# Q and out with eight heads on 128 partitions: 8 KB rows and an accumulated pair of matmuls in a linear attention kernel

## The chip, the core and the metric

One core of one Trainium2 chip. The metric is device time of one launch in microseconds (us). The profiled span runs from the first to the last instruction and is 1.7 to 1.9 us shorter than the timed run. With one core there is no other core to compare a run with; where a run is marked slow below, it lies over 1.5% above the fastest of its kernel. All ratios use fast runs.

## The reference

```python
batch, heads, seq, dim = 8, 12, 512, 64          # 96 heads, fp32
Q_feat, K_feat = np.maximum(0, Q), np.maximum(0, K)
KV    = np.einsum('bhkd,bhkv->bhdv', K_feat, V)  # 64x64 per head
K_sum = np.sum(K_feat, axis=2)
out   = einsum(Q_feat, KV) / (einsum(Q_feat, K_sum)[..., None] + 1e-10)
```

Q, K and V are 12.6 MB each, so is the output: 50.3 MB pass through the DMA engines, for little arithmetic.

## The kernel before

Four heads make a group; there are 24. GpSimd issues the loads, which cast fp32 to bf16 on the way. In Q and out each partition holds 16 positions of a head, 1024 values: rows of 4 KB in HBM. K and V rows are 2 KB. A group goes through VectorE (ReLU of K, V into a block-diagonal tile), TensorE (KV with a column of ones for the denominator), ScalarE (KV to bf16), TensorE (Q transposed), ScalarE (ReLU), TensorE (the product, one matmul per 32 output partitions) and VectorE (two normalizations of 128x512), then a store.

```python
# ... loads: K, V, Q of each group in turn; the last two Q at the very end
def mm_out(g):
    for j in range(2):
        po = pou.tile([P, 2, 512], fp32, name="ps_out")
        ps_out[g, j] = po
        for v in range(U // 2):
            u = j * (U // 2) + v
            for h in range(NHG):                      # four heads, 32 partitions each
                hs = slice(32 * h, 32 * h + 32)
                nc.tensor.matmul(po[hs, ...], qt[g][:, u, hs],
                                 kvd[g % NB][:, h // 2, h % 2, :, :], start=True, stop=True, ...)
# ...
for g in range(NG):
    mm_kv(g); evac_kv(g)
    if g + 1 < NG:
        prep(g + 1)                                   # ReLU of K, V copies (VectorE)
    if g > 0:
        mm_out(g - 1)
        store(g - 1, norm(g - 1))                     # groups 17 to 21: queued behind the loads
    transp(g); evac_qt(g)
mm_out(NG - 1)
store(NG - 1, norm(NG - 1))                           # in two halves
```

## Time and profile before

| | before |
|---|---|
| time, median | 131.77 us (131.31 to 132.03, four runs) |
| profiled span | 130.2 us |
| DMA packets, HBM bytes | 20126; 50.3 MB |
| TensorE matmuls, mean granted clock | 1344; 0.81 |
| last load packet ends | 119.9 us |
| VectorE ends its last normalization | 126.07 us |

The page cuts the span into 40 slices and gives each a digit for how busy an engine was; groups of instructions carry the busy time, the mean of one, and what ended the idle time before them. The packet records of the trace are read beside it: each has a queue, a size, a start and a duration, and they give the time of the last load. They are put on the span's clock to about 0.2 us. The queue that carries the engines' instructions is a line that the prediction passed over:

```profile
q8 instruction: 10, 0.16, 0.5%
```

Ten packets of 16 KB: the program itself is read by DMA.

### The profile page before, as it was taken

The numbers are of one execution on the slowest core, as the hardware profiler recorded it, in microseconds if no ns is written. First come the engines' busy times: TensorE is split into PE (matmuls) and PEld (weight loads), VectorE is DVE, ScalarE is ACT, GpSimd is POOL, SyncE is SP. The second block draws the span as 40 slices with busy tenths as digits, with TensorE's granted clock in tenths as the row PEclk, the third lists the DMA queues.
The fourth block names the chain that finished last, engine by engine and source line by source line (L and its number), as shares of the span: only waits on it lengthen the run. The fifth ranks groups of instructions, "written<-read, shape, count | busy, mean of one in ns | idle before, by whom it ended". The sixth has DMA issues, their size and how long they took to land.

```text
span 130.2 us, 3249 instructions
## 1 busy us (share of the span) xinstructions
PE 75.7 (58%) x1344; PEld 62.8 (48%) x1344; DVE 90.3 (69%) x228; ACT 43.7 (34%) x73; POOL 51.4 (39%) x81
## 2 busy tenths in 40 slices
PE   0057975648475574763843943954757658959510
PEld 0057863536455454543733832843745546757300
DVE  4388995837577577577685775775866859979860
ACT  1205554152323523423343244235132352535500
POOL 6986451414434335144344353352433433312100
PEclk9999999586865797698699599599596586777985
DMA  3999999999999999999999999999999999999982
GB/s 122 301 208 208 203 195 218 306 223 278 216 272 257 232 285 242 247 285 218 271 274 216 285 253 236 286 235 255 281 213 279 266 223 207 204 217 374 380 322 89
DMA packets 20126, 32.18 MB, mean 247 GB/s; under 512 B 1552, under 2 KB 13328, under 8 KB 20112
## 3 DMA queue, kind: packets, MB, share of 16 engines
q0 software_dynamic: 16688, 20.98, 87.3%
q1 hardware_dynamic: 3152, 10.49, 21.4%
q10 hardware_dynamic: 272, 0.52, 1.1%
q8 instruction: 10, 0.16, 0.5%
q14 instruction: 4, 0.03, 0.1%
HBM read 37.75 MB, written 12.58 MB: 387 GB/s over the span
## 4 chain that ended last, share of the span: by engine, by line
DMA 79%; DVE 7%; POOL 5%; issue 3%; PE 1%; ACT 1%; ACTq 0%; POOLq 0%
DMA v_sb<-in_V_dram 37%; DMA k_sb<-in_K_dram 23%; DMA q_sb<-in_Q_dram 19%; DVE o_sb L172 3%; DVE vbd L120 2%; POOL v_sb L83 2%; POOL k_sb L81 2%; DVE rec L171 1%; POOL q_sb L87 1%; ACT qt L147 1%; DVE den L169 1%; PE ps_out L158 1%; DVE kf L114 0%; PE ps_qt L143 0%; POOL ident masks.py:199 0%
## 5 line engine op out<-in xcount | busy, mean ns | idle before, releaser
L128 PE MATMUL ps_kv<-vbd,kf 128*128 128x130 bf16 x384 | 36.8, 270 | 40.1 <-DVE vbd L120 40.1
L128 PEld LDWEIGHTS <-kf 128*128 128x128 bf16 x384 | 33.6, 124 | 42.3 <-issue 28.6
L137 ACT CAST kvd<-ps_kv 64x260 bf16<-64x260 f32 x48 | 17.9, 374 | 49.6 <-PE ps_kv L128 49.0
L172 DVE TENSOR_TENSOR o_sb<-ps_out,rec 128x512 f32<-128x512 f32 x48 | 33.2, 692 | 1.7
L147 ACT ACTIVATE qt<-ps_qt 128x1024 bf16<-128x1024 bf16 x24 | 24.6, 1023 | 27.4 <-PE ps_qt L143 27.3
L120 DVE COPY vbd<-v_sb 64x1024 bf16<-64x1024 bf16 x46 | 19.9, 432 | 12.8 <-DMA v_sb<-in_V_dram 12.5
L158 PE MATMUL ps_out<-kvd,qt 128*32 128x130 bf16 x768 | 23.2, 271 | 8.2 <-DVE o_sb L172 5.3
L87 POOL DMA_DIRECT2D q_sb<-in_Q_dram x24 | 13.6, 565 | 31.3 <-DMA k_sb<-in_K_dram 30.2
L114 DVE TENSOR_SCALAR kf<-k_sb 128x2048 bf16<-128x2048 bf16 x23 | 16.0, 696 | 13.3 <-DMA k_sb<-in_K_dram 13.2
L81 POOL DMA_DIRECT2D k_sb<-in_K_dram x23 | 17.1, 743 | 18.6 <-DMA v_sb<-in_V_dram 16.7
L158 PEld LDWEIGHTS <-qt 128*32 128x32 bf16 x768 | 15.2, 115 | 15.0 <-DVE o_sb L172 7.8
L83 POOL DMA_DIRECT2D v_sb<-in_V_dram x23 | 17.3, 752 | 10.9 <-DMA q_sb<-in_Q_dram 9.2
L143 PE MATMUL ps_qt<-ident,q_sb 128*128 128x128 bf16 x192 | 18.8, 256 | 0.1
L143 PEld LDWEIGHTS <-q_sb 128*128 128x128 bf16 x192 | 14.2, 116 | 3.9 <-issue 2.6
L171 DVE RECIPROCAL rec<-den 128x8 f32<-128x8 f32 x48 | 9.8, 203 | 1.6
L169 DVE TENSOR_SCALAR den<-ps_out 128x8 f32<-128x8 f32 x48 | 7.7, 161 | 1.3 <-PE ps_out L158 0.6
L182 POOL DMA_DIRECT2D out_dram<-o_sb x5 | 2.9, 579 | 9.5 <-DVE den L169 2.8
L105 DVE MEMSET vbd<- 128x1040 f32 x3 | 2.8, 925 | 1.6 <-PEq L221 1.0
L114 DVE TENSOR_SCALAR kf<-k_first 128x2048 bf16<-128x2048 f32 x1 | 1.2, 1228 | 2.7 <-DMA k_first<-in_K_dram 2.7
L137 ACT ACT_TABLE_LOAD x1 | 1.3, 1283 | 2.8 <-DVE kvd L108 2.8
L120 DVE CAST vbd<-v_first 64x1024 bf16<-64x1024 f32 x2 | 1.4, 706 | 0.0
L108 DVE MEMSET kvd<- 128x260 f32 x3 | 0.8, 275 | 0.3
(7 smaller groups left out, 1.3 us busy)
## 6 DMA issues: line engine op xcount, KB each, us to landing
out_dram<-o_sb SPq DMA_DIRECT2D x18, 512.0 KB, 6.2
q_sb<-in_Q_dram POOLq DMA_DIRECT2D x24, 256.0 KB, 12.5
k_sb<-in_K_dram POOLq DMA_DIRECT2D x23, 256.0 KB, 13.8
v_sb<-in_V_dram POOLq DMA_DIRECT2D x23, 256.0 KB, 13.9
out_dram<-o_sb POOLq DMA_DIRECT2D x5, 512.0 KB, 9.1
v_first<-in_V_dram ACTq DMA_DIRECT2D x1, 512.0 KB, 4.9
k_first<-in_K_dram SPq DMA_DIRECT2D x1, 512.0 KB, 4.6
out_dram<-o_sb SPq DMA_DIRECT2D x2, 256.0 KB, 3.3
```

What stands on the lines that cost most here:

```text
L81: nc.gpsimd.dma_start(out=k_sb[g].rearrange("p j r d -> p j (r d)"), in_=Kr[g])
L83: nc.gpsimd.dma_start(out=v_sb[g].rearrange("p j r d -> p j (r d)"), in_=Vr[g])
L87: nc.gpsimd.dma_start(out=q_sb[g].rearrange("p u f -> p (u f)"), in_=Qr[g])
L114: nc.vector.tensor_scalar(kf[g].rearrange("p j r c d -> p (j r) c d"), k_sb[g].rearrange("p j r d -> p (j r) d").unsqueeze(2).to_broadcast ...
L120: nc.vector.tensor_copy(vbd[g % NB][hs, :, :, h, 0:D].rearrange("p j r d -> p (j r) d"), v_sb[g][hs].rearrange("p j r d -> p (j r) d"))
L128: nc.tensor.matmul(ps_kv[g][:, j, :, :], kf[g][:, j, r, :, :].rearrange("p c d -> p (c d)"), vbd[g % NB][:, j, r, :, :], start=(r == 0), s ...
L137: nc.scalar.copy(kvd[g % NB][ts_, :, :, t, :].rearrange("p j h d -> p (j h) d"), ps_kv[g][ts_].rearrange("p j h d -> p (j h) d"))
L143: nc.tensor.transpose(ps_qt[g][:, u, :], q_sb[g][:, u, :], ident)
L147: nc.scalar.activation(qt[g].rearrange("p u q -> p (u q)"), ps_qt[g].rearrange("p u q -> p (u q)"), Act.Relu)
L158: nc.tensor.matmul(po[hs, v // 2, (v % 2) * 2 * D1:(v % 2) * 2 * D1 + 2 * D1], qt[g][:, u, hs], kvd[g % NB][:, h // 2, h % 2, :, :], start ...
L171: nc.vector.reciprocal(rec, den)
L172: nc.vector.tensor_tensor(o_sb[:, 8 * j:8 * j + 8].rearrange("p (b r) d -> p b r d", b=2), pv[:, :, :, 0:D], rec.unsqueeze(3).to_broadcast ...
```

## The change

The intent is fewer and longer DMA packets. Eight heads (an octet) share 128 partitions, 16 each, so a Q or output row is 8 KB. A 32-partition slice of transposed Q then holds two heads with different KV. The change writes transposed Q twice, into tiles where the odd heads' or the even heads' columns are zero, and accumulates two matmuls per 32 columns. KV's buffers go from 3 to 4, three octets instead of five groups have their stores queued behind the loads, and products run half an octet at a time. Some smaller edits are not in the cut below and are not tested by themselves: K and V get 18 on-chip buffers each instead of 20, results 5 of double size instead of 10, and K and V of group 1 are loaded ahead of the first Q.

```diff
-    RQ = S * 4 // P
+    RQ = S * 8 // P
-    HELD = 5
+    HELD = 3
+    qtf = [consts.tile([P, 2, U * P], bf16, name=f"qt{i}") for i in range(NZ)]   # zeroed once
...
-        nc.scalar.activation(qt[g]..., ps_qt[g]..., Act.Relu)
+        for z in range(2):
+            nc.scalar.activation(qtz[o % NZ][:, z, us, :, z, :], pv[:, :, :, z, :], Act.Relu)
...
-                for h in range(NHG):
+            for z in range(2):
+                for w in range(4):
+                    h = 2 * w + z
                     nc.tensor.matmul(
                         po[hs, ...],
-                        qt[g][:, u, hs],
+                        qtf[o % NZ][:, z, u * P + 32 * w:u * P + 32 * w + 32],
-                        start=True, stop=True, ...
+                        start=(z == 0), stop=(z == 1), ...
...
+    for o in range(NO + 1):
+        for i in range(2):
+            g = 2 * o + i
+            # mm_kv(g), evac_kv(g), prep(g + 1)
+            if o > 0:
+                for j in (2 * i, 2 * i + 1):
+                    mm_out(o - 1, j)
+                    norm(o - 1, j, o_sb[o - 1])
+                # store(o - 1) after its fourth norm; the last octet in quarters
+            if o < NO:
+                transp(o, i)
+                evac_qt(o, i)
```

More of the change, by code (lines that the diff above doesn't have):

```diff
@@ L32 @@
     NG = NH // NHG
-    assert NG * NHG == NH and R == 8 and RQ == 16
-    HELD = 5
+    NO = NG // 2
+    assert NO * 8 == NH and R == 8 and RQ == 32
+    HELD = 3
     fp32 = mybir.dt.float32
@@ L44 @@
     consts = pool("consts", 1)
-    qin = pool("qin", NG)
-    kin = pool("kin", 20)
-    vin = pool("vin", 20)
+    qin = pool("qin", NO)
+    kin = pool("kin", 18)
+    vin = pool("vin", 18)
     kfp = pool("kfp", 3)
-    qtp = pool("qtp", 3)
     rcp = pool("rcp", 4)
-    outp = pool("outp", 10)
+    outp = pool("outp", 5)
     pkv = pool("pkv", 2, space=bass.MemoryType.PSUM)
@@ L66 @@
     NB = 3
+    NK = 4
+    NZ = 2
     vbf = [consts.tile([P, PR * R * 2 * D1], bf16, name=f"vbd{i}") for i in range(NB)]
-    kvf = [consts.tile([P, PR * 2 * 2 * D1], bf16, name=f"kvd{i}") for i in range(NB)]
+    kvf = [consts.tile([P, PR * 2 * 2 * D1], bf16, name=f"kvd{i}") for i in range(NK)]
     vbd = [x.rearrange("p (j r h d) -> p j r h d", j=PR, r=R, h=2) for x in vbf]
+    qtf = [consts.tile([P, 2, U * P], bf16, name=f"qt{i}") for i in range(NZ)]
+    qtz = [x.rearrange("p z (u w y c) -> p z u w y c", u=U, w=4, y=2) for x in qtf]
     kvd = [x.rearrange("p (j h t d) -> p j h t d", j=PR, h=2, t=2) for x in kvf]
@@ L83, in load_kv, with load_q @@
         nc.gpsimd.dma_start(out=v_sb[g].rearrange("p j r d -> p j (r d)"), in_=Vr[g])
-    def load_q(g):
-        q_sb[g] = qin.tile([P, U, 2 * D], bf16, name="q_sb")
-        nc.gpsimd.dma_start(out=q_sb[g].rearrange("p u f -> p (u f)"), in_=Qr[g])
+    def load_q(o):
+        q_sb[o] = qin.tile([P, U, 2 * D], bf16, name="q_sb")
+        nc.gpsimd.dma_start(out=q_sb[o].rearrange("p u f -> p (u f)"), in_=Qr[o])
     k_sb[0] = outp.tile([P, PR, R, D], fp32, name="k_first", tag="o_sb")
@@ L93, with zero_q @@
     nc.scalar.dma_start(out=v_sb[0].rearrange("p j r d -> p j (r d)"), in_=Vr[0])
+    load_kv(1)
     load_q(0)
     make_identity(nc, ident)
-    for g in range(1, NG - 2):
-        load_kv(g)
-        load_q(g)
-    load_kv(NG - 2)
-    load_kv(NG - 1)
-    load_q(NG - 2)
-    load_q(NG - 1)
+    for o in range(1, NO):
+        load_kv(2 * o)
+        load_kv(2 * o + 1)
+        load_q(o)
     def zero(i):
-        nc.vector.memset(vbf[i].bitcast(fp32), 0.0)
-        for h in range(2):
-            nc.vector.memset(vbd[i][64 * h:64 * h + 64, :, :, h, D:D1].rearrange("p j r o -> p (j r) o"), 1.0)
+        if i < NB:
+            nc.vector.memset(vbf[i].bitcast(fp32), 0.0)
+            for h in range(2):
+                nc.vector.memset(vbd[i][64 * h:64 * h + 64, :, :, h, D:D1].rearrange("p j r o -> p (j r) o"), 1.0)
         nc.vector.memset(kvf[i].bitcast(fp32), 0.0)
-    kf, qt, ps_kv, ps_qt, ps_out = {}, {}, {}, {}, {}
+    def zero_q(i):
+        nc.vector.memset(qtf[i].rearrange("p z f -> p (z f)").bitcast(fp32), 0.0)
+    kf, ps_kv, ps_qt, ps_out = {}, {}, {}, {}
     def prep(g):
@@ L136, in evac_kv @@
             ts_ = slice(64 * t, 64 * t + 64)
-            nc.scalar.copy(kvd[g % NB][ts_, :, :, t, :].rearrange("p j h d -> p (j h) d"),
+            nc.scalar.copy(kvd[g % NK][ts_, :, :, t, :].rearrange("p j h d -> p (j h) d"),
                            ps_kv[g][ts_].rearrange("p j h d -> p (j h) d"))
-    def transp(g):
-        ps_qt[g] = pqt.tile([P, U, P], bf16, name="ps_qt")
-        for u in range(U):
-            nc.tensor.transpose(ps_qt[g][:, u, :], q_sb[g][:, u, :], ident)
-    def evac_qt(g):
-        qt[g] = qtp.tile([P, U, P], bf16, name="qt")
-        nc.scalar.activation(
-            qt[g].rearrange("p u q -> p (u q)"), ps_qt[g].rearrange("p u q -> p (u q)"), Act.Relu)
@@ L150, in mm_out, with transp @@
-    def mm_out(g):
-        for j in range(2):
-            po = pou.tile([P, 2, 512], fp32, name="ps_out")
-            ps_out[g, j] = po
-            for v in range(U // 2):
-                u = j * (U // 2) + v
-                for h in range(NHG):
-                    hs = slice(32 * h, 32 * h + 32)
+    def transp(o, i):
+        ps_qt[o, i] = pqt.tile([P, U // 2, P], bf16, name="ps_qt")
+        for u in range(U // 2):
+            nc.tensor.transpose(ps_qt[o, i][:, u, :], q_sb[o][:, i * (U // 2) + u, :], ident)
@@ new lines, in evac_qt, with mm_out @@
+    def evac_qt(o, i):
+        us = slice(i * (U // 2), (i + 1) * (U // 2))
+        pv = ps_qt[o, i].rearrange("p u (w y c) -> p u w y c", w=4, y=2)
+        for z in range(2):
+            nc.scalar.activation(qtz[o % NZ][:, z, us, :, z, :], pv[:, :, :, z, :], Act.Relu)
+    def mm_out(o, j):
+        po = pou.tile([P, 2, 512], fp32, name="ps_out")
+        ps_out[o, j] = po
+        for v in range(4):
+            u = 4 * j + v
+            for z in range(2):
+                for w in range(4):
+                    hs = slice(32 * w, 32 * w + 32)
+                    h = 2 * w + z
@@ L158, in mm_out @@
                     nc.tensor.matmul(
                         po[hs, v // 2, (v % 2) * 2 * D1:(v % 2) * 2 * D1 + 2 * D1],
-                        qt[g][:, u, hs],
-                        kvd[g % NB][:, h // 2, h % 2, :, :],
-                        start=True, stop=True, skip_group_check=True)
-    def norm(g):
-        o_sb = outp.tile([P, RQ, D], fp32, name="o_sb", tag="o_sb")
-        for j in range(2):
-            pv = ps_out[g, j][:, :, 0:4 * D1].rearrange("p b (r d) -> p b r d", d=D1)
-            den = rcp.tile([P, 2, 4], fp32, name="den")
-            nc.vector.tensor_scalar(den, pv[:, :, :, D], scalar1=1e-10, scalar2=None, op0=Alu.add)
-            rec = rcp.tile([P, 2, 4], fp32, name="rec")
-            nc.vector.reciprocal(rec, den)
-            nc.vector.tensor_tensor(
-                o_sb[:, 8 * j:8 * j + 8].rearrange("p (b r) d -> p b r d", b=2),
-                pv[:, :, :, 0:D],
-                rec.unsqueeze(3).to_broadcast([P, 2, 4, D]), op=Alu.mult)
-        return o_sb
@@ L180, in store @@
-    def store(g, o_sb):
-        if NG - 2 - HELD <= g < NG - 2:
-            nc.gpsimd.dma_start(out=Or[g], in_=o_sb.rearrange("p r d -> p (r d)"))
-        elif g == NG - 1:
-            for j in range(2):
-                rs = slice(RQ // 2 * j, RQ // 2 * (j + 1))
-                nc.sync.dma_start(out=Or[g].rearrange("p (r d) -> p r d", d=D)[:, rs],
-                                  in_=o_sb[:, rs])
-        else:
-            nc.sync.dma_start(out=Or[g], in_=o_sb.rearrange("p r d -> p (r d)"))
+                        qtf[o % NZ][:, z, u * P + 32 * w:u * P + 32 * w + 32],
@@ new lines, in mm_out, with norm @@
+                        kvd[(2 * o + h // 4) % NK][:, h % 4 // 2, h % 2, :, :],
+                        start=(z == 0), stop=(z == 1), skip_group_check=True)
+    def norm(o, j, o_sb):
+        pv = ps_out[o, j][:, :, 0:4 * D1].rearrange("p b (r d) -> p b r d", d=D1)
+        den = rcp.tile([P, 2, 4], fp32, name="den")
+        nc.vector.tensor_scalar(den, pv[:, :, :, D], scalar1=1e-10, scalar2=None, op0=Alu.add)
+        rec = rcp.tile([P, 2, 4], fp32, name="rec")
+        nc.vector.reciprocal(rec, den)
+        nc.vector.tensor_tensor(
+            o_sb[:, 8 * j:8 * j + 8].rearrange("p (b r) d -> p b r d", b=2),
+            pv[:, :, :, 0:D],
+            rec.unsqueeze(3).to_broadcast([P, 2, 4, D]), op=Alu.mult)
@@ L191, with store, store_quarter @@
+    def store(o, o_sb):
+        if NO - 1 - HELD <= o < NO - 1:
+            nc.gpsimd.dma_start(out=Or[o], in_=o_sb.rearrange("p r d -> p (r d)"))
+        else:
+            nc.sync.dma_start(out=Or[o], in_=o_sb.rearrange("p r d -> p (r d)"))
+    def store_quarter(o, j, o_sb):
+        rs = slice(8 * j, 8 * j + 8)
+        nc.sync.dma_start(out=Or[o].rearrange("p (r d) -> p r d", d=D)[:, rs], in_=o_sb[:, rs])
     zero(0)
     prep(0)
-    for g in range(NG):
-        mm_kv(g)
-        evac_kv(g)
-        if g + 1 < NG:
-            if g + 1 < NB:
-                zero(g + 1)
-            prep(g + 1)
-        if g > 0:
-            mm_out(g - 1)
-            store(g - 1, norm(g - 1))
-        transp(g)
-        evac_qt(g)
@@ L205 @@
-    mm_out(NG - 1)
-    store(NG - 1, norm(NG - 1))
+    zero_q(0)
+    o_sb = {}
+    for o in range(NO + 1):
+        for i in range(2):
+            g = 2 * o + i
+            if o < NO:
+                mm_kv(g)
+                evac_kv(g)
+                if g + 1 < NG:
+                    if g + 1 < NK:
+                        zero(g + 1)
+                    prep(g + 1)
+                if o == 0 and i == 0:
+                    zero_q(1)
+            if o > 0:
+                if i == 0:
+                    o_sb[o - 1] = outp.tile([P, RQ, D], fp32, name="o_sb", tag="o_sb")
+                for j in (2 * i, 2 * i + 1):
+                    mm_out(o - 1, j)
+                    norm(o - 1, j, o_sb[o - 1])
+                    if o == NO:
+                        store_quarter(o - 1, j, o_sb[o - 1])
+                if i == 1 and o < NO:
+                    store(o - 1, o_sb[o - 1])
+            if o < NO:
+                transp(o, i)
+                evac_qt(o, i)
```

## The prediction

> **What bounds the kernel now.** I read the page first: the slices, the DMA queues, the chain that ended last. Then the windows (busy time by stretch), the waits, and the timeline of the last 20 us.
>
> ```profile
> DMA  3999999999999999999999999999999999999982
> DMA packets 20126, 32.18 MB, mean 247 GB/s; under 512 B 1552, under 2 KB 13328, under 8 KB 20112
> q0 software_dynamic: 16688, 20.98, 87.3%
> q1 hardware_dynamic: 3152, 10.49, 21.4%
> HBM read 37.75 MB, written 12.58 MB: 387 GB/s over the span
> DMA 79%; DVE 7%; POOL 5%; issue 3%; PE 1%; ACT 1%; ACTq 0%; POOLq 0%
> ```
>
> The 16 DMA engines are full from the second slice to the last but one, and 79% of the final chain is loads that follow one another. q0 carries the loads that cast fp32 to bf16 (and five late stores), q1 the other stores. The shares add to over 100% because packet records overlap. Bytes are counted at the destination here; on the fp32 side it is 50.3 MB, 387 GB/s.
>
> ```profile
> 24.00:40.00 16.00, 10.32 (x168) 8.35 (x168) 10.25 (x26) 5.05 (x9) 5.55 (x10) 0.71 1.16 254
> 8.00:24.00 16.00, 11.89 (x193) 10.22 (x192) 12.88 (x33) 7.08 (x12) 8.12 (x13) 0.98 1.17 213
> ...
> DVE kf L114 <- DMA k_sb<-in_K_dram: 13.2, 16, 1.5
> DVE vbd L120 <- DMA v_sb<-in_V_dram: 12.5, 18, 1.5
> ```
>
> The columns of the first two are PE, PEld, DVE, ACT, POOL, granted clock, DMA share, GB/s. In steady state no engine is busy for over 65% to 70% of a stretch, and DVE waits in most groups for K and again for V. So the middle is bound by DMA. The end is not:
>
> ```profile
> 118.20 0.85 DVE L120 COPY vbd<-v_sb 64x1024 bf16<-64x1024 bf16 x2
> 119.08 0.17 DVE L169 TENSOR_SCALAR den<-ps_out 128x8 f32<-128x8 f32 x1
> ...
> 123.91 0.17 DVE L169 TENSOR_SCALAR den<-ps_out 128x8 f32<-128x8 f32 x1 [0.58 <-PE ps_out L158]
> ...
> 125.38 0.69 DVE L172 TENSOR_TENSOR o_sb<-ps_out,rec 128x512 f32<-128x512 f32 x1
> ```
>
> After the last V copy DVE runs six normalizations with one gap of 0.6 us, ends at 126.07, and the last store takes the 4.1 us to 130.2. In the trace's packet records the last K/V packet ends at about 117.5 and the last Q packet at about 120.0, so the end is **last load + 6.1 + 4.1**.
>
> **What the Trainium skill says.** "DMA: Bandwidth & Descriptors", section "Issuing engines are not separate DMA queues": all transfers run on the same 16 engines and interleave. The trace agrees: with q0 and q1 together the DMA share stays at 1.16. The same page, section "Why small descriptors are slow (HBM only)", gives each packet a small fixed cost, about 3 cycles. The packet records agree in sign: a K or V row (2 KB read, 1 KB written) takes 98 ns, a Q row (4 KB read) 174 ns, not 196; a store row of 2 KB 84 ns, of 4 KB 160 ns. "TensorE: Matmul & The Clock Gate", Part 1: the array is at half clock by default and activity releases it. The windows agree: 0.98 where PE is busy 11.9 of 16 us, 0.71 where it is 10.3. "ScalarE: Activation LUTs", section "What ACT_TABLE_LOAD costs": an activation with immediates takes 186 ns + 0.833 ns per column, 1039 for 1024; the trace has 1023.
>
> **The change part by part.**
>
> Bytes are the same. Q loads go from 24 with 4 KB rows to 12 with 8 KB rows (3072 packets to 1536), stores from 25 to 15, with 8 KB rows but for the last four. Records overlap, so what counts is the time an engine needs from one packet to the next. I fitted this from packet counts in 3 us stretches of the steady part: about 81 ns for a K/V row, 150 for a Q row, 163 for a 4 KB store. From 81 at 2 KB and 150 at 4 KB the fixed part is about 12 ns and each 2 KB about 69, so an 8 KB Q row should take about 288 ns against 2 x 150. Gains before the last load lands:
> - Q: 1536 x 12 ns / 16 engines = 1.2 us.
> - Stores: 84 and 160 ns leave 8 ns fixed; some 1024 packets saved x 8 / 16 = 0.5 us.
> - Completion packets (4 bytes, 19 ns in the records): 12 loads and 9 stores fewer, 21 x 16 x 19 / 16 = 0.4 us.
> - Stores held behind the loads: before, groups 17 to 21 (2.6 MB) were held, the program stored 17 x 0.52 MB ahead; now octets 8 to 10 (3.1 MB) are held and 8 x 1.05 MB go ahead. That is 0.5 MB less ahead of the last load, 128 x 163 / 16 = 1.3 us. It is moved, not removed.
>
> Sum 3.4 us: the last load lands near 116.6, not 120.0.
>
> PE: the product with KV doubles, since the zero halves are multiplied too:
>
> ```profile
> L158 PE MATMUL ps_out<-kvd,qt 128*32 128x130 bf16 x768 | 23.2, 271 | 8.2 <-DVE o_sb L172 5.3 <-DVE den L169 1.4 <-ACT qt L147 1.4
> L128 PE MATMUL ps_kv<-vbd,kf 128*128 128x130 bf16 x384 | 36.8, 270 | 40.1 <-DVE vbd L120 40.1
> L147 ACT ACTIVATE qt<-ps_qt 128x1024 bf16<-128x1024 bf16 x24 | 24.6, 1023 | 27.4 <-PE ps_qt L143 27.3
> ```
>
> 23.2 us / 768 = 30 ns of busy time each, so 768 more cost 23 us: PE 75.7 to about 99 of 130 us. That lies beside DMA: PE idles 40 us for DVE, which waits for V. Per octet at full clock (timeline: 1.09 for 16 KV matmuls, 0.62 for 8 transposes, 0.41 per 16 of the product) PE needs 2 x 1.09 + 2 x 0.62 + 4 x 0.82 = 6.7 us, at half clock (1.89, 1.03, 1.06 per 32) 10.1. An octet's data takes about 10 us with its store and 7.8 in the last stretch without. By the clock page more work should hold the clock up, so PE should just keep up.
>
> DVE: the same prep and normalization (3.6 us per group of 5.1), plus two memsets of 128x2048 fp32; from 925 ns for 1040 columns, 1.8 us each, 3.6 in all, during the start where loads run ahead. ACT: 48 activations of 512 columns, by the skill's rule 612 ns, 29.4 us instead of 24.6; ACT was 34% busy. POOL issues 12 loads fewer (6.8 us); not the bound.
>
> **The tail grows.** Two things change. Q of the last octet lands last (1 MB, 2.6 us after V of group 23), and the program's first transpose of that octet stands ahead of the KV matmuls of group 23. And eight normalizations now follow the last V copy, not six. Counting from the last load: transposes 0.6, KV matmuls 1.2 to 1.9, 32 product matmuls 0.8, so the third of those eight starts at about +2.8 (the first two are done by +1.5, and DVE idles between). Six follow at 1.04 us (timeline: 119.08, 120.13, 121.17), to +9.1, where before it was +6.1. Then 4.1 us for the last store. So the span is 116.6 + 9.1 + 4.1 = 129.8, against 130.2: **3.4 us gained by DMA, 3.0 given back by the tail**. The held 3.1 MB need some 8 us at 400 GB/s, of which 2 MB can start with the last load, so they should be gone before the last store.
>
> The timed runs are 1.4 us over the span (131.63 to 130.2), so 131.2; I put 131.1, since a warmer PE may shorten the tail by a few tenths.
>
> **The rivals.**
> - *Rows of 8 KB are much cheaper than fitted.* The plain record durations (98 and 174) give a fixed 22 ns, so 2.1 us from Q and not 1.2; with a lucky tail 128.5. For it: those are the records. Against: the stretch with only loads already moves about 413 GB/s of fp32, and any mix moves 397 to 415, which looks like a limit in bytes.
> - *Rows are cut at 4 KB.* Then only the completion packets and the held store remain (1.7 us) and the tail loses 3: about 133. Against it: the program issues single 8 KB rows.
> - *PE becomes the bound in the last octets*, at half clock 10.1 us against 7.8, which would add 2 us or more a stage: 133 to 135. For it: a clock that alternates between half and full. Against: busier stretches had the higher clock.
> - *Hidden:* stores of 8 KB packets starve the 2 KB loads in bursts. Sum of bytes and rate stay, so only the arrival of loads moves: 0 to 0.5 us.
>
> **Range and chances.** Gain of 1.7 to 4.5 us by DMA, loss of 2.5 to 5 by the tail: from about 128.8 to 133.6. Faster by over 2% (under 129.0) needs the large gain and the small loss together: 0.14. Slower by over 2% (over 134.3) needs PE to fall behind or cut rows: 0.08.
>
> **What would show it.** Page: the packets of Q halve in number (now 4 KB written each), and the sum of shares of q0 and q1 falls by 2 to 3 points; packets of 8 KB appear in q1. PE near 99 us, clock over 0.81. In the timeline the last load lands near 116 to 117 and DVE ends some 9 us later, with a gap of about a microsecond ahead of the third of the last eight normalizations. The waits of DVE for K and V stay in the middle. I am wrong if the packets stay as many, if the clock falls and PE's idle time goes, or if the last load lands over 2 us from 116.6.

## The result, and the profile after

The changed kernel took **133.58 us** (133.28 to 134.11, four runs) against 131.77: ratio **1.0146**, 95% interval 1.0101 to 1.019. The ratios are those of the record, from the fast runs of both kernels in the same rounds, so not quite the ratios of the medians. It is a loss of 1.5%, where a gain of about half a per cent was forecast. Later, beside other runs, the same kernel gave 1.0121 (1.0099 to 1.0142). The profile shown here is of its slowest run (134.11); the later one, of 133.14, is nearer its median, and both are used.

The DMA part of the page of the changed kernel, with GB/s counted at the destination:

```profile
DMA  4999999999999999999999999999999999995591
GB/s 124 286 213 198 213 203 210 207 204 236 317 226 346 214 204 349 232 250 317 215 202 340 240 199 327 249 194 244 330 209 229 327 225 208 261 354 215 238 344 59
DMA packets 16964, 32.28 MB, mean 244 GB/s; under 512 B 1200, under 2 KB 12976, under 8 KB 15536
q0 software_dynamic: 14672, 21.50, 85.2%
q1 hardware_dynamic: 2000, 9.96, 19.3%
q8 instruction: 16, 0.26, 0.7%
```

Packets fell by 3162 and the shares of q0 and q1 by 4.2 points. But the DMA engines now have two half-empty slices near the end, and there are 16 instruction packets for 10. The groups of instructions that the change touched:

```profile
L171 PE MATMUL ps_out<-kvd,qt 128*32 128x130 bf16 x1536 | 34.1, 245 | 10.8 <-issue 7.7
L159 ACT ACTIVATE qt<-ps_qt 128x512 bf16<-128x512 bf16 x48 | 26.0, 594 | 47.9 <-PE ps_qt L153 47.9
L117 DVE MEMSET qt<- 128x2048 f32 x2 | 3.5, 1765 | 1.0 <-issue 1.0
```

The doubled product shows a wait that it did not have: 7.7 us for "issue", which is time in which the engine waited for nothing that the profile shows. The list of waits has it on the weight loads too (total us, times, longest); in the kernel before, the product's weight loads had 4.9 us of it, 0.3 us at the longest, and its matmuls none:

```profile
PEld L171 <- issue: 13.0, 20, 2.1
PE ps_out L171 <- issue: 7.7, 6, 1.9
```

The end, in VectorE's timeline (start, duration, and in brackets the idle time before it and who ended it):

```profile
116.71 0.85 DVE L129 COPY vbd<-v_sb 64x1024 bf16<-64x1024 bf16 x2
117.60 0.17 DVE L180 TENSOR_SCALAR den<-ps_out 128x8 f32<-128x8 f32 x1
...
120.38 0.17 DVE L180 TENSOR_SCALAR den<-ps_out 128x8 f32<-128x8 f32 x1 [0.62 <-PE ps_out L171]
...
123.60 0.17 DVE L180 TENSOR_SCALAR den<-ps_out 128x8 f32<-128x8 f32 x1 [1.05 <-PE ps_out L171]
...
127.14 0.69 DVE L183 TENSOR_TENSOR o_sb<-ps_out,rec 128x512 f32<-128x512 f32 x1
```

Eight normalizations after the last V copy, a gap of 0.62 us ahead of the third as forecast, and one of 1.05 us ahead of the last four that was not. The chain of work that ended last says what the second gap is:

```profile
121.66 0.47 PE ps_out L171 x20
122.13 1.06 issue
123.19 0.39 PE ps_out L171 x12
```

TensorE stops in the middle of a product, after 20 of its 32 matmuls, and no semaphore holds it. An instruction packet starts at 121.45 in the packet records and takes 0.93 us; TensorE goes on 1.7 us after that start.

The three terms of the forecast sum, on the packet records and timelines of both profiles of the changed kernel:

| | before | forecast | after, 134.11 us run | after, 133.14 us run |
|---|---|---|---|---|
| last load packet ends | 119.9 | 116.6 | 118.3 | 117.2 |
| from there to VectorE's end | 6.2 | 9.1 | 9.5 | 10.0 |
| from there to the end of the span | 4.1 | 4.1 | 4.5 | 4.2 |
| span | 130.2 | 129.8 | 132.3 | 131.4 |

The DMA engines moved 402.8 GB/s on the fp32 side between 12 and 108 us before, and 407.7 and 407.9 after. The two profiles of one kernel differ by 1.1 us in the last load, so a difference of that size between two profiles says little by itself.

### The profile page after: what moved, and what is told of

Read it like the earlier page. It is cut to its first block, busy times and chain, and to the rows that moved or that the text cites. A ratio compares the mean times of both kernels' runs of the same rounds, so it can differ in the third digit from the quotient of the medians.

```text
span 132.3 us, 4779 instructions
## 1 busy us (share of the span) xinstructions
PE 81.8 (62%) x2112; PEld 70.7 (53%) x2112; DVE 93.1 (70%) x231; ACT 44.4 (34%) x97; POOL 45.5 (34%) x67
## 4 chain that ended last, share of the span: by engine, by line
DMA 79%; PE 7%; issue 4%; DVE 4%; POOL 2%; POOLq 0%
DMA v_sb<-in_V_dram 32%; DMA k_sb<-in_K_dram 25%; DMA q_sb<-in_Q_dram 21%; PE ps_out L171 3%; PE ps_kv L137 3%; DVE o_sb L183 3%; PE ps_qt L153 2%; POOL k_sb L88 1%; DVE rec L182 1%; DVE den L180 1%; POOL q_sb L94 0%; POOL ident masks.py:199 0%; POOL ident masks.py:197 0%; POOL v_sb L90 0%; POOLq L240 0%
## 5 line engine op out<-in xcount | busy, mean ns | idle before, releaser
L137 PE MATMUL ps_kv<-vbd,kf 128*128 128x130 bf16 x384 | 35.0, 261 | 22.2 <-DVE vbd L129 22.2
L137 PEld LDWEIGHTS <-kf 128*128 128x128 bf16 x384 | 30.9, 119 | 23.7 <-DVE vbd L129 15.0
L159 ACT ACTIVATE qt<-ps_qt 128x512 bf16<-128x512 bf16 x48 | 26.0, 594 | 47.9 <-PE ps_qt L153 47.9
L171 PE MATMUL ps_out<-kvd,qt 128*32 128x130 bf16 x1536 | 34.1, 245 | 10.8 <-issue 7.7
L171 PEld LDWEIGHTS <-qt 128*32 128x32 bf16 x1536 | 27.6, 109 | 16.8 <-issue 13.0
L153 PE MATMUL ps_qt<-ident,q_sb 128*128 128x128 bf16 x192 | 17.6, 244 | 11.7 <-DMA q_sb<-in_Q_dram 11.1
L153 PEld LDWEIGHTS <-q_sb 128*128 128x128 bf16 x192 | 12.9, 109 | 15.0 <-DMA q_sb<-in_Q_dram 12.6
L94 POOL DMA_DIRECT2D q_sb<-in_Q_dram x12 | 7.9, 660 | 18.2 <-DMA v_sb<-in_V_dram 18.2
L191 POOL DMA_DIRECT2D out_dram<-o_sb x3 | 2.0, 683 | 15.6 <-DVE o_sb L183 15.6
L117 DVE MEMSET qt<- 128x2048 f32 x2 | 3.5, 1765 | 1.0 <-issue 1.0
```

Of the source, the lines that this page charges most:

```text
L137: nc.tensor.matmul(ps_kv[g][:, j, :, :], kf[g][:, j, r, :, :].rearrange("p c d -> p (c d)"), vbd[g % NB][:, j, r, :, :], start=(r == 0), s ...
L153: nc.tensor.transpose(ps_qt[o, i][:, u, :], q_sb[o][:, i * (U // 2) + u, :], ident)
L159: nc.scalar.activation(qtz[o % NZ][:, z, us, :, z, :], pv[:, :, :, z, :], Act.Relu)
L171: nc.tensor.matmul(po[hs, v // 2, (v % 2) * 2 * D1:(v % 2) * 2 * D1 + 2 * D1], qtf[o % NZ][:, z, u * P + 32 * w:u * P + 32 * w + 32], kvd[ ...
```

## The experiments

Theory: the longer rows do raise the DMA rate; the doubled product costs time at the end, because PE stops for instructions; and the coarser octet leaves more work, and a hole in the DMA traffic, after the last load. Rivals: the rows are worth nothing; PE's work lies beside DMA at the end as well; the wait for Q or the late stores are the whole loss. Kernels are edits of the changed kernel unless said otherwise, and ratios are to the kernel before.

### Rows cut at 4 KB

```diff
-        q_sb[o] = qin.tile([P, U, 2 * D], bf16, name="q_sb")
+        q_sb[o] = qin.tile([P, 2, U * D + 32], bf16, name="q_sb")    # a gap in the row
-        nc.gpsimd.dma_start(out=q_sb[o].rearrange("p u f -> p (u f)"), in_=Qr[o])
+        nc.gpsimd.dma_start(out=q_sb[o][:, :, 0:U * D], in_=Qr[o].rearrange("p (j f) -> p j f", j=2))
# the same for o_sb and the stores
```

> The changed kernel with Q rows and output rows cut into two packets of 4 KB each by a gap in the on-chip tile; the number of transfers, the matmuls and the order are as in the changed kernel (ratio to before 1.0146, last load packet near 118.3 us). Theory A (8 KB rows do cost less per byte; they raised the DMA rate by 1.2%): last load 1.0 to 1.5 us later, ratio 1.020 to 1.026. Rival (the DMA engines are bound by bytes, the rows are worth nothing): last load within 0.4 us of 118.3 and ratio 1.011 to 1.018.

Measured: 135.47 us, ratio **1.0278** (1.0247 to 1.0309). The page of this kernel:

```profile
DMA packets 19908, 32.28 MB, mean 240 GB/s; under 512 B 1200, under 2 KB 12976, under 8 KB 19888
```

The rate from 12 to 108 us is 403.3 GB/s, that of the kernel before. So the long rows alone raise it by 1.1%, and taking them away costs 1.3% to 1.6% of the time. The last load ended at 118.6, which is 0.3 to 1.4 us later than in the two profiles of the changed kernel: the ratio exceeded the range, the last load just met it at one end. With rows as before, it still ended 1.3 us before the kernel before's 119.9; that fits the 1.3 us forecast for the store bytes moved behind it. A part of the loss of time is not the rows': TensorE's stop in the tail was 1.66 us in this profile, against 1.06 and 1.21. By the rate alone the rows are worth 1.3 us. The rival falls: the rows are worth about what was hoped, and the loss lies elsewhere.

### Half of the product

```diff
-            for z in range(2):
+            for z in range(1):          # wrong result on purpose
-                        start=(z == 0), stop=(z == 1), ...
+                        start=(z == 0), stop=True, ...
```

> The changed kernel with only the first of the two accumulated matmuls (a wrong result on purpose: odd heads' rows are missing), so PE has 1344 matmuls as before. Theory (the doubled product costs at the end: PE's instruction fetches, 16 of 16 KB instead of 10, stop it for 1.06 us in the tail, and 32 matmuls stand where 16 stood): instruction packets back to 10 or 11, one gap of about 1 us ahead of the last four normalizations gone or shorter, 1.0 to 1.8 us less than the changed kernel, ratio 1.001 to 1.007. Rival (PE lies beside DVE and DMA, also in the tail): under 0.4 us, ratio 1.011 to 1.0146.

Measured: 131.31 us, ratio **0.9998** (0.9978 to 1.0019), with a wrong result (20 of 22 runs were fast; most lie between 131.1 and 131.6). Its page and the last gap in VectorE's timeline:

```profile
q8 instruction: 10, 0.16, 0.5%
```

```profile
118.36 0.17 DVE L180 TENSOR_SCALAR den<-ps_out 128x8 f32<-128x8 f32 x1 [0.67 <-PE ps_out L171]
```

The instruction packets are back to 10, the gap of 0.67 us for Q remains, and the one ahead of the last four is gone. VectorE ends 8.1 us after the last load. The second matmul costs 1.2% to 1.5%, somewhat more than expected. Not all of it lies in the tail: the last load ended at 116.5, which is 0.7 to 1.8 us before the changed kernel's, and less of the held stores had gone past by then (0.34 MB against 0.49 and 0.76).

### Instructions or array time

```diff
+                    n = 2 * D1 if z == 0 else 2     # wrong result on purpose
                     nc.tensor.matmul(
-                        po[hs, v // 2, (v % 2) * 2 * D1:(v % 2) * 2 * D1 + 2 * D1],
+                        po[hs, v // 2, (v % 2) * 2 * D1:(v % 2) * 2 * D1 + n],
```

> The changed kernel with the second of the two accumulated matmuls cut to 2 columns of 130 (a wrong result on purpose): as many PE instructions and fetches (16) as the changed kernel, half of the product's array time. Theory (instructions and their fetches cost it): the gap of about 1 us ahead of the last four normalizations stays, ratio 1.009 to 1.0146. Rival (array time costs it): the gap shrinks, ratio 0.998 to 1.005, as halfmm.

Measured: 133.23 us, ratio **1.0116** (1.0098 to 1.0135), wrong result. TensorE's timeline of this kernel:

```profile
122.69 0.62 PE L172 MATMUL ps_out<-kvd,qt 128*32 128x2 bf16 x44 [1.55 <-issue]
```

Half of the array's work on the product is gone and nothing is gained: the stop stays, and so does the time. The cost goes with the number of TensorE instructions (a weight load and a matmul each), not with the columns that they stream.

### The doubled product in the kernel before

```diff
# kernel before
+                for z in range(2):                  # every matmul twice, same values
                     for h in range(NHG):
```

> The kernel before with every matmul of the product issued twice (the second overwrites the first with the same values; the result is right): 2112 matmuls as in the changed kernel, everything else as before. Theory (the doubled product costs about 1.4% by itself, through PE's stops in the tail): 16 instruction packets, ratio 1.008 to 1.018. Rival (it costs only in the changed kernel, whose last octet leaves PE less room): ratio 0.998 to 1.004.

Measured: a correct result, 134.18 us median of six, ratio of the fast runs **1.0122** (1.0074 to 1.017). Three of six runs were marked slow, the profiled one among them, so its profile is used only for what kind of stop there is. Its chain of work:

```profile
121.14 0.58 PE ps_out L159 x28
121.72 1.80 issue
123.53 0.69 PE ps_out L159 x36
```

It has 16 instruction packets as well. The doubling costs 1.2% in the old layout, too, by three runs of which one (132.28) stands apart: the other five lie between 133.78 and 134.84, so that 1.2% is rather too low than too high.

### Moving the stop

```diff
+    ps_d = pkv.tile([P, PR, 2, D1], fp32, name="ps_d", tag="ps_kv")
+    for x in range(88):                             # or 117; ahead of the first KV product
+        nc.tensor.matmul(ps_d[0:32, 0, 0, 0:32], ident[:, 0:32], ident[:, 0:32], start=True, stop=True, ...)
```

In the tail of the changed kernel two stops are 127 matmuls apart (after 53 of the 64 at 115.9 us, then after 11 + 8 + 16 + 64 + 8 + 20 more). That is 254 instructions. By the page 16 packets come for the 4224 instructions of TensorE, and 10 for 2688 before: 264 to 269 a packet, as an estimate. If the stop belongs to the place in the instruction stream, small matmuls early in the program must move it.

> The same with 88 small matmuls, which move the fetches 40 matmuls later: the stop should fall into the third product from the front of the last eight, on which DVE waits. Theory (fetch): the gap ahead of the third of the last eight normalizations grows from 0.6 to 1.5 us or more, the one ahead of the last four goes; the sum of gaps, and the time, stay near the changed kernel's (1.011 to 1.018). Rival (operands): gaps where they were.

> The changed kernel with 117 small matmuls (32x32, result overwritten) ahead of the first KV product, where PE is idle. They move PE's instruction fetches, one for every 128 matmuls, 11 matmuls later in the tail: the stop comes while PE waits for the last Q load and again after a whole product of the last octet. Theory (PE stops 1.06 us where its fetched instructions end, and this is on the path): the gap ahead of the last four normalizations shrinks from 1.05 us to 0.7 or less and lies ahead of the last three; DVE ends 0.4 to 1.0 us earlier against the last load; ratio 1.006 to 1.012. Rival (the gap belongs to the wait for octet 11's operands): the gap stays ahead of the last four; ratio 1.0146 +- 0.003.

> The changed kernel again (a blank line added), as a control for the others of this call and to see how far the last load and the tail move from one profiled run to the next. Expected: ratio 1.0146 +- 0.004; last load packet between 117.2 and 118.4 us; DVE ends some 9.5 us after it; a gap of about 1 us ahead of the last four normalizations.

Measured: after2 (the changed kernel unchanged) 1.0121 (1.0099 to 1.0142); shift88 133.44 us, **1.0129** (1.0109 to 1.0148); shift117 133.31 us, **1.0128** (1.0093 to 1.0162). VectorE's timeline of shift88, then GpSimd's with the store of octet 10:

```profile
119.63 0.17 DVE L180 TENSOR_SCALAR den<-ps_out 128x8 f32<-128x8 f32 x1 [0.58 <-PE ps_out L171]
...
121.70 0.15 DVE L180 TENSOR_SCALAR den<-ps_out 128x8 f32<-128x8 f32 x1
122.74 0.15 DVE L180 TENSOR_SCALAR den<-ps_out 128x8 f32<-128x8 f32 x1
```

```profile
122.08 0.53 POOL L191 DMA_DIRECT2D out_dram<-o_sb  x1 [5.55 <-DVE den L180]
```

In shift88 the gap ahead of the last four normalizations went, but the stop that I expected in the third product did not come: there is none in the tail. VectorE ended at 125.92, 1.3 us before after2, and yet the span was 131.7 against 131.4. So **another path of nearly the same length** ends this kernel. As the trace reads, it is that of the last line: the store of octet 10, 1 MB in one transfer, issued at 122.08, when its fourth normalization is done. By the windows of its trace (where packets stand some 0.3 us early) the DMA engines moved 229, 74 and 0 GB/s in the microseconds from 120 to 123, then had 2 MB of stores left, which at 400 GB/s is 5 us.

In shift117 there was no stop in the tail either, but a gap of 2.32 us ahead of the third normalization. The windows of that kernel (columns as in the prediction) say why:

```profile
118.00:121.00 3.00, 3.00 (x60) 2.80 (x61) 0.77 (x2) 1.83 (x4) 0.00 (x0) 0.50 0.76 317
```

The granted clock was 0.50 there, after TensorE had idled for Q; the KV product took 1.94 us and not 1.10. What was gained at one place was lost at another. Both placements missed their expected gaps. That the stop moves with the instruction count came out as expected; what it costs at its new place was not foreseen.

The kept traces say more than the two placements. All 82 stops of TensorE over 0.15 us that are marked "issue" (15 kernels; the kernel before and halfmm have none) come ahead of the same matmuls, counted from the program's start with the small ones: 222, 349 or 350, 477, 604, 731 or 732, and so on to 1877, 2004 and 2132, in steps of some 127 or a multiple of it. And all 82 end 1.7 to 2.2 us after the start of an instruction packet. So these stops are waits for instructions. In shift88 the boundary at matmul 2004 lay in the tail as well (119.0 us), but its packet had started at 116.7, while TensorE waited for Q, and nothing stopped.

What no run shows is a kernel that has these instructions, no stop in its tail and nothing else changed, and is faster for it. That the instructions cost the time is shown by halfmm against thinmm; that they cost it through these stops is how the traces read.

### Stores held until the last load has landed

```diff
+        if o == NO - 1 - HELD:
+            nc.gpsimd.tensor_copy(gate, q_sb[NO - 1][:, 0, 0:2])   # waits for the last Q
         if NO - 1 - HELD <= o < NO - 1:
```

> The changed kernel with the three held stores issued only after the last Q load has landed (a copy of two columns of it by GpSimd stands ahead of the first). Theory (0.76 MB of the first held store went past before the last load and cost it the 1.3 us that I had counted on): last load at 116.3 to 116.9, DVE ends 1.2 to 1.9 us earlier, ratio 1.000 to 1.006. Rival 1 (the last load is not delayed by that store): no change, 1.0146 +- 0.003. Rival 2 (the stores are now what ends last): last load earlier, but ratio at or over 1.0146.

Measured: 134.65 us, ratio **1.0214** (1.0188 to 1.024). The last load ended at 117.35 and VectorE at 125.89, but the span at 133.1: my second rival. The slices of its page:

```profile
DMA  3999999999999999999999999999999999729990
GB/s 131 262 212 196 217 199 213 204 204 282 289 248 324 212 304 263 214 227 341 214 202 362 218 284 280 212 204 347 232 201 324 252 204 209 147 97 419 376 362 18
```

The engines fall empty at the last load (97 GB/s in the 36th slice), because the first packet of the first store ends only 1.8 us after its issue at 117.97; after that they run full to the end. Here the bytes left over set the end, whatever VectorE does. A held store fills the gap between the last load and the first fresh results, and taking it away is dear.

This run also bears on the stop. Its program has the same TensorE instructions as the changed kernel, and yet the first product of octet 11, which stops there after 20 matmuls, runs through:

```profile
120.88 0.65 PE L172 MATMUL ps_out<-kvd,qt 128*32 128x130 bf16 x32 [0.31 <-DVE den L181]
```

Its instruction packet had started at about 118.1, when the DMA engines were nearly idle, and not at 120.4 to 121.4 as in the two profiles of the changed kernel.

### The last transposes behind the products

```diff
                     norm(o - 1, j, o_sb[o - 1])
+                    if o == NO - 1 and i == 1:
+                        transp(o, j - 2); evac_qt(o, j - 2)
-            if o < NO:
+            if o < NO - 1:
                 transp(o, i)
```

> The changed kernel with the last octet's transposes moved: the KV matmuls of group 23 no longer stand behind the transpose that waits for the last Q load, and the two halves of the transposes follow the third and fourth product of octet 10. Theory (the wait for Q in PE's order costs the tail): the gap of 0.6 us ahead of the third of the last eight normalizations goes and part of the next; DVE ends 0.8 to 1.8 us earlier, ratio 1.001 to 1.009. Rival (the tail is eight normalizations and a fetch stop, whatever the order): within 0.4 us, ratio 1.011 to 1.018.

Measured: 132.74 us, ratio **1.0074** (1.0056 to 1.0093), 0.5% to 0.7% better than the changed kernel and inside the expected range. The gap for Q is gone; the stop ahead of the last four is now longer in VectorE's timeline:

```profile
123.06 0.17 DVE L180 TENSOR_SCALAR den<-ps_out 128x8 f32<-128x8 f32 x1 [1.84 <-PE ps_out L171]
```

### Both paths at once

```diff
-                    if o == NO:
+                    if o >= NO - 1:                  # octet 10 in quarters too
                         store_quarter(o - 1, j, o_sb[o - 1])
-                if i == 1 and o < NO:
+                if i == 1 and o < NO - 1:
                     store(o - 1, o_sb[o - 1])
```

split10_shift88 adds the 88 small matmuls to this, and split10_order_shift88 the late transposes as well.

> The changed kernel with the store of octet 10 cut into four quarters, each issued by SP as soon as its normalization is done (as octet 11's are), instead of one 1 MB store by GpSimd after the fourth. Theory (two paths of near equal length: the hole in the DMA traffic after 120 us, and DVE's end): the hole fills, the last store no longer queues behind 1 MB, and the span ends 2.6 to 3.3 us after DVE instead of 4.2: ratio 1.001 to 1.008. Rival (DVE's chain alone sets the end): 1.010 to 1.0146.

> Both: quarters for octet 10, and the 88 small matmuls that take PE's stop off the path. Theory of two paths: shift88 alone gave nothing, here it gives its 1.0 to 1.3 us: ratio 0.989 to 0.998. Rival (the stop costs nothing, the hole alone did): as split10.

> These two and the moved transposes of the last octet (order). Theory: the gap of 0.6 us ahead of the third of the last eight normalizations goes as well, so 0.3 to 0.7 us less than split10_shift88, if PE's stop does not come back in the new order: ratio 0.984 to 0.995, the best version that the experiments point to. Rival (the bytes left over now set the end): no better than split10_shift88.

Measured: split10 132.93 us, **1.01** (1.0068 to 1.0132), hardly better than after2, against an expected 1.001 to 1.008; split10_shift88 132.76 us, **1.0087** (1.0058 to 1.0117); split10_order_shift88 132.59 us, **1.0077** (1.0053 to 1.0101). The hole filled (never under 318 GB/s from 117 to 123 us in the windows of split10's trace), but the stop came back where shift88 had driven it out. TensorE's timeline of split10_shift88:

```profile
123.75 0.78 PE L171 MATMUL ps_out<-kvd,qt 128*32 128x130 bf16 x36 [1.53 <-issue]
```

In shift88 the packet for that place started at 120.4, into thinning traffic (229 GB/s in that microsecond); here it started at 121.8, with the engines busy. That fits a fetch that stands in line with the data, and the packet records on file agree. After a stop, the next instruction packet started 3.8 to 4.8 us later in all 63 cases where the DMA share until then was 1.05 or more, and some 1.4 us later in the two where the engines were nearly empty (hold at 116.6 us, bothcut at 124.2; share 0.1 or less). In between it took 2.0 to 4.2 us. No run varies the queue alone, so this is a reading of traces. These three missed their expectation.

### The last heads as before

> A version that should beat both: 8 KB rows for octets 0 to 10; the last two groups as in the kernel before (4 KB rows, one matmul per 32 columns, Q last); transposes after the third and fourth product in all octets, so that no KV matmul waits for Q; the last three K/V preparations behind the normalizations that are ready. Theory (8 KB rows raise the DMA rate by about 1.2%, and what they lost was the longer tail): last load near 117.4 us, DVE ends 5.5 to 7 us after it, no stop of PE on the path, ratio 0.980 to 0.992. Rival (the end is set by the bytes of stores left over, 3.5 to 4 MB after the last load): DVE ends early but the span does not: ratio 0.992 to 1.005.

> The hybrid (last two groups as in the kernel before) with octet 10 stored in quarters. The hybrid's DVE ended at 127.1 us after a gap of 2.4 us that PE's stop and the late transposes left; its span was 130.5. Theory: little to gain in this one, since its stores were not what ended last (3.4 us after DVE): ratio 0.996 to 1.002. Rival (the hole in DMA traffic mattered here too): 0.985 to 0.994.

> 8 KB rows with doubled products for octets 0 to 9, the last 16 heads in four groups with the loads, order, products and stores of the kernel before. Theory (row length raises the DMA rate; the tail is that of the kernel before: DVE ends some 6.2 us after the last load and the span 4.1 us later): last load at 116.8 to 117.8 us, ratio 0.978 to 0.990, the best version. Rival (the loss lies in the steady part, or the stores left over set the end): ratio 0.995 to 1.005.

In hybrid the last two groups have the old layout, and the order around them is changed, with the late transposes of order for all octets; in hybrid_split octet 10 is stored in quarters as well.

```diff
-    for o in range(NO + 1):
+    for o in range(NO - 1):                          # octets; last Q rows of 4 KB
...
+    prep(NG - 2); half(0); half(1)                   # half(j): products and norm j of octet 10
+    mm_kv(NG - 2); evac_kv(NG - 2); prep(NG - 1); half(2); half(3)
+    store(a, o_sb[a])                                # hybrid_split: a quarter in each half(j)
+    mm_kv(NG - 1); evac_kv(NG - 1)
+    last_transp(NG - 2); last_transp(NG - 1)
+    # then products of one matmul, norms and stores of groups NG - 2 and NG - 1
```

Measured: 132.31 us, **1.0022** (1.0003 to 1.0041; 16 of 22 runs fast), and 132.6 us, **1.0044** (1.0021 to 1.0067; 20 of 22). Better than the changed kernel by 1%, but outside the expected ranges, and both still have octet 10's doubled product after the last-but-one V, with a stop in it.

hybrid4 goes back to the old layout for the last 16 heads, with the old order of loads, products and stores:

```diff
-    for o in range(1, NO):
+    for o in range(1, NO - 2):
         load_kv(2 * o); load_kv(2 * o + 1); load_q(o)          # 8 KB rows
+    for g in (NG - 4, NG - 3): load_kv(g); load_qg(g)          # 4 KB rows
+    load_kv(NG - 2); load_kv(NG - 1); load_qg(NG - 2); load_qg(NG - 1)
...
+    for g in (NG - 2, NG - 1):
+        mm_kv(g); evac_kv(g)
+        if g + 1 < NG: prep(g + 1)
+        group(g - 1)                   # products of one matmul, two norms, store
+        last_transp(g)
+    group(NG - 1)
```

Measured: **130.87 us** (130.43 to 130.97, six runs), ratio **0.993** (0.9912 to 0.9949), a correct result. It beats both kernels, by 0.7% and 2%, though less than expected. Its last load ended at 117.4 us, 2.5 before the kernel before's, and TensorE's longest wait after 115 us is for transposed Q, as before:

```profile
123.22 0.64 PE L213 MATMUL ps_out<-kvd,qtl 128*32 128x130 bf16 x32 [1.17 <-ACT qtl L204]
```

The 2.5 us are not all kept: VectorE, which has four normalizations to catch up with from octet 9 and group 20, runs without a gap from 112.3 to 123.1 us and ends at 125.86, only 0.2 us before the kernel before's. The rest of the gain is in the last stores: the span ends 3.1 us after VectorE, against 4.1.

## Why the prediction was wrong

- *DMA is the bound, the tail belongs to VectorE.* Right; it holds after the change.
- *Q rows, stores and completions gain 2.1 us.* Right in kind, too large in size: the rate rose by 1.2%, which over 117 us is 1.4 us, and bothcut shows that nearly all of it is the rows. The fixed part of a packet that I fitted is not tested by itself; the plain durations (an 8 KB Q row took 329 ns on average, against 2 x 174) would have said more. For the stores I had misread them: 160 ns was the mean of the five late ones, while those in the middle took 172 ns for 4 KB and 324 for 8 KB, so the 8 ns had no ground.
- *0.5 MB of stores moved behind the last load, 1.3 us.* Supported by bothcut (1.3 us), though the profile of the 134.11 us run lost part of it: 0.76 MB of held stores had gone past before its last load, against 0.49 in the 133.14 us run. The last load lands at 118.3 or 117.2, not 116.6.
- *"PE should just keep up", and the 23 us lie beside DMA.* **This is the step that failed.** The array does keep up: the clock rose from 0.81 to 0.89, as I had expected from the Trainium skill ("TensorE: Matmul & The Clock Gate", Part 1; thinmm, with less work for the array, had 0.81 to 0.84), and 1536 matmuls were busy for 34.1 us, not 46.4. But I counted the array's time and not the instructions. 768 more matmuls are 1536 more instructions, which come in six more DMA packets, and TensorE stopped at their boundaries, for 1.06 us on the final chain of the first profile. halfmm (0.9998), thinmm (1.0116) and before_double (1.0122) show that the doubling costs 1.2% to 1.5%, and that it is the count of instructions. Without the second matmul the forecast sum comes out: halfmm's last load at 116.5, VectorE 8.1 us later and a span of 129.5, against 116.6, 9.1 and 129.8. I had forecast a ratio of 0.995, so of the 2% that I missed the doubling is the larger part. (The two windows that I set beside that page show less than I made of them: the same table has 0.87 where PE was busy 9.1 of 16 us. And the window 8:24 has VectorE at 80%, over the 65% to 70% that I wrote.)
- *The tail: +9.1.* The eight normalizations, their 1.04 us and the gap ahead of the third were right (that gap came at +2.1 and not +2.8); the stop adds the rest of 9.5 and 10.0.
- *The held stores "should be gone before the last store".* They were, but too early: the next one comes late and whole, and 2 MB then queue. In shift88 VectorE ended 1.3 us earlier and the span was no shorter, so a second path ends as late. That it is this store is read from the trace; storing it in quarters alone (split10) gave 0.2% to 0.5%, hardly more than the noise.
- *Rivals.* Much cheaper rows: not at the rate seen. Rows cut at 4 KB: no, the trace has 8 KB packets. PE as the bound in the last octets: right that TensorE would be at fault, wrong in the way, since the clock did not fall overall. Hidden: not tested; the rate in the middle rose, so no loss by it shows.
- *Range and signs.* The range does not follow from its terms: 131.6 - 4.5 + 2.5 and 131.6 - 1.7 + 5 give 129.6 to 134.9, not 128.8 to 133.6. The signs that I had named for being wrong stayed away (packets fell, the clock rose, the last load was within 2 us of 116.6), since none of them looked at instructions.

In sum, rows bring about 1.4%, the doubled product takes about as much, and what is left, which I put down to the octet's longer tail, takes as much again: with half of the product the changed kernel is back at the time of the kernel before, although its rows are longer. How the last part divides between the wait for Q (0.5% to 0.7% by order), the coarse store and the two additional normalizations is not settled, since the paths run side by side and the single edits do not add up.

## What to carry to other kernels

When a change adds instructions to an engine that streams short ones, count the instructions and their fetches, not the busy time alone: here stops of 0.6 to 1.9 us stood in the middle of the changed kernel too, where the DMA engines were full all the same, and the one at 122 us lay on the final chain. A larger unit of work that pays in the steady part can lengthen the tail, as the octet did here; giving the last units the old, finer form, as in hybrid4, was worth 2%. And where mending one path moves its end but not the span, look for a second path before judging the first.

## What the Trainium skill lacked or had wrong

- "Runtime: NRT & Kernel Launch", section "Instruction fetch mechanics", says that instructions come in 16 KiB blocks of 256, and that the fetch is mostly hidden. The blocks agree (16 packets for the changed kernel, stops 127 matmuls apart); hidden they are not always: with pairs of weight load and 130-column matmul at some 20 ns a pair (32 in 0.65 us), TensorE stopped seven times in the changed kernel, for 0.6 to 1.9 us. And the page does not say that the fetch waits behind data: after a stop the next packet started 3.8 to 4.8 us later beside full DMA engines, 1.4 us beside empty ones.
- "DMA: Bandwidth & Descriptors", section "Why small descriptors are slow (HBM only)", speaks of small descriptors only. Here rows of 8 KB for half of the bytes still raised the rate from 403.3 to 407.9 GB/s against 4 KB rows.
- "DMA: Bandwidth & Descriptors", section "Latency and other measured facts", gives about 1 us to the first byte for transfers that GpSimd issues. In hold a store issued into nearly empty DMA queues at 117.97 us had its first packet start at about 119.4 and end at 119.73 us, 1.4 and 1.76 us later.
